# A two-layer decoder step on one core: side steps, weight splits and norms get other due times

## The chip, the cores and the metric

The kernel runs on one core of a Trainium2 chip. Its time is device time in microseconds (us) from launch to end; three runs of the kernel before took 2095.05, 2097.28 and 2099.48 us, median 2097.28. Engines: TensorE (PE, with its weight loads PEld), VectorE (DVE), ScalarE (ACT), GpSimd (POOL), and SyncE (SP), which here only issues DMAs.

## The reference, cut to what matters

One inference step of two layers for 1024 prompt positions and 8 single-position samples, together 1032 columns, all in float32 with a model width of 1024.

```python
def layer(x, ...):
    h = modulate(rmsnorm(x, g_mix), sh1, sc1)
    q, k, v, g, u, vv = split(h @ w_in)            # 4 heads x 128 each of q k v g, 4 groups x 128 each of u vv
    q, k = rope(q), rope(k) * 128 ** -0.5
    o, s_new = retention(q, k, v, s_ret)           # chunks of 128, decayed, state S carried on
    o_ret = silu(g) * group_norm(o) * gain
    o_gm = gelu(u) * (W_s @ layer_norm(gelu(vv)) + b_s)     # inside chunks of 128
    x = x + gt1 * (concat(o_ret, o_gm) @ w_out)
    h2 = modulate(rmsnorm(x, g_ffn), sh2, sc2)
    a = causal_dwconv3(h2 @ w_up)                  # 2 x 2048 columns
    x = x + gt2 * ((silu(a1) * a2) @ w_down)
# shifts, scales and gates (sh, sc, gt) are silu(c) @ w_ada + b_ada; two layers, then a last rmsnorm
```

## The kernel before, in words

Channels lie on partitions, the 1032 columns on the free axis in three chunks of 344. Every large product runs in three parts (`mm3`, L261): weights and activations are each split into a high part rounded for TensorE (`hi`, made on ScalarE, L212) and the rest (`lo`, made on VectorE, L221), and hi x hi, hi x lo and lo x hi are summed in PSUM. The three matmuls of one 128 x 128 weight tile are called a triple here.

A **unit** (L273) computes 128 output channels: three chunks of 8 triples, 24 in all. After each chunk VectorE evicts it from PSUM and multiplies by the norm's row factor R (L292); at the unit's end an eviction function `evac` works on the row. A layer has the value and key of head 0 in a **joint** (L296, two outputs at once, chunks in the order 2, 0, 1, evicted by ScalarE), then the query and gate of head 0, four units of head 1, two of group 0, two of group 1; an output product over three of the results (`partial`); heads 2 and 3, groups 2 and 3; another `partial`; and a `final_partial` (L511), which ends the residual chunk by chunk and sends each chunk's norm off while the next is computed. The feed-forward part is a joint and 30 units, in pairs, with partial products in between. That makes 52 units a layer.

**Side steps.** All smaller work is written as generators, `Task`s, which the planner `Side` (L55) lets go on between the triples. A unit calls `side.tick(KB)` after every third triple and at its end; that adds 1.31 to a clock that exists at build time only, and runs the next step of up to two tasks that are due, in the order of their priority and age. `yield y` makes a task's next step due y later; a task whose `after` is unfinished waits. In a joint a tick comes after each triple and counts as a third. So the planner sets only the order in which each engine's instructions stand; at run time an engine goes on as soon as its data are there. Instructions of one engine run in this order.

A head's tasks: `task_v` transposes v (L707, L630) and loads the old states; `task_k` rotates k (L675 to L677), transposes it (L630) into kt, scaled on ScalarE (L730), multiplies kt with v (L743) and sums the states S on VectorE; `task_q` rotates q, makes the masked scores `at` (L773) and the output o (L794, L796) and normalises it in `row_norm` (statistics L642, scale L645 to L654, normalise L657); `task_o` transposes o and os (L815, L630), multiplies by the gate and splits the result `mix`. Each of k, q and o comes after the ones before it. At the end of the key's and the query's units `rope_evac` puts three copies on ScalarE (L668 to L670). A group has `task_v` (transposes L850 and L630, the same row_norm, transpose of the last rows L858) and `task_s` (product with W_s, L873).

**Weights.** `Weights.ahead()` (L232) does what is next for the following unit: the low half of the piece whose high half is there, and the high half of the next. `high()` also issues the load of a piece two further on SyncE's queue. A unit calls it at triples 9, 15 and 21. Whatever is missing at the next unit's start is made then.

**Norms.** `norm` (L439) of a chunk: add the squares (VectorE, L378), sum over channels by matmul (`inv_rms`, L396, then a root on VectorE), write the factor to DRAM on GpSimd's queue, and read it back to all partitions on SyncE's. The three chunks' norms follow each other by `after`; the second has a wait of 8 at its head.

All these tiles share a pool of 23 buffers (`slot`), and all PSUM tiles eight banks. In layer 0 the conditioning weights (`ada`, product L590) pass through the same pool, at the lowest priority.

Of the kernel before, what the change touches and what calls it, by code (L numbers as in the profile page):

```python
# [41 lines left out]
ORDER = (2, 0, 1)  # L42
# [48 lines left out]
def tile_hybrid_decoder_step(  # L91
# [57 lines left out]
    for l in range(DEPTH):  # L149
# [15 lines left out]
        out, down = list(rows(w_out, OUT_GROUPS)), list(rows(w_down, DOWN_GROUPS))  # L165
# [107 lines left out]
    def unit(evac, R):  # L273

        u = W.get()
        a, b = None, small([128, 1], "wb", 4)
        for c in range(NC3):
            n, s = chunk(c, 2)
            ps = big()
            for k in range(KT):  # L280
                hi, lo = W.tile(u, k)
                mm3(ps[:, 0:n], hi, lo, Hh[:, k, s], Hl[:, k, s], k == 0, k == KT - 1)
                i = c * KT + k + 1
                if i in (9, 15, 21):
                    W.ahead()
                if i % 3 == 0 and i < NC3 * KT:
                    side.tick(KB)
            if c == 0:
                a = slot("row")
            if c == NC3 - 1:  # L290
                nc.scalar.activation(out=b, in_=ps[:, CW:CW + 1], func=ACTF.Copy)  # L291
            nc.vector.tensor_tensor(out=a[:, cols(c)], in0=ps[:, 0:CW], in1=R[:, cols(c)], op=ALU.mult)  # L292
        evac((a, b))
        side.tick(KB)
# [141 lines left out]
            late.append(lambda x=x, a=a, m=m: nc.vector.scalar_tensor_tensor(  # L436
                out=Hl[:, m, s], in0=x, scalar=a, in1=Hhf[:, m, s], op0=ALU.mult, op1=ALU.subtract))

    def norm(c, hold, R, A, B, gate=None, dma=True):  # L439

        n = CW if c < 2 else CW - NB
        if c == ORDER[1] and B is not mods[0][0]:
            yield 8
        rows = add_squares(c, hold, gate)
        yield 4
        w = inv_rms(rows)
        yield 4
        if dma:
            rd = to_dram(w)
        if c == 2 or not dma:  # L450
            r = spread(w, (3,) if dma else range(4))
        yield 1
        o = R[:, c * CW:c * CW + n]
        if dma:
            from_dram(o, rd)
        else:
            nc.scalar.activation(out=o, in_=r[:, 0:n], func=ACTF.Copy)
        if c == 2:
            q = small([128, KT, NB], "gs")
            ss = slice(SEQ, T)  # L460
            rb = r[:, CW - NB:CW].unsqueeze(1).to_broadcast([128, KT, NB])
            nc.vector.tensor_tensor(out=q, in0=XS, in1=rb, op=ALU.mult)
            nc.vector.tensor_tensor(out=q, in0=q, in1=A[:, :, 1:9], op=ALU.mult)
            nc.vector.tensor_tensor(out=q, in0=q, in1=B[:, :, 1:9], op=ALU.add)
            nc.scalar.activation(out=Hh[:, :, ss], in_=q, func=ACTF.Copy)
            nc.vector.tensor_tensor(out=Hl[:, :, ss], in0=q, in1=Hhf[:, :, ss], op=ALU.subtract)
# [44 lines left out]
    def final_partial(acts, gt, A, B=None, out=None):  # L511

        u = W.get(lazy=1)
        K = len(acts)
        norms = []
        R = None
        if out is None:
            R = rows_scale()
            columns(B)
        for o, c in enumerate(ORDER):  # L520
            n = CW if c < 2 else CW - NB
            s = slice(c * CW, (c + 1) * CW)
            hold, late = [], []
            for ms in GROUPS3:
                pss = {}
                mk = [(m, k) for m in ms for k in range(K)]
                if o == 0 and ms[0] == 0:
                    mk.sort(key=lambda q: q[1])
                for i, (m, k) in enumerate(mk):
                    hi, lo = W.tile(u, m * K + k)  # L530
                    if k == 0:
                        pss[m] = big()
                    ps = pss[m]
                    mm3(ps[:, 0:CW], hi, lo, acts[k][0][:, s], acts[k][1][:, s], k == 0, k == K - 1)
                    if k == K - 1:
                        xs = X[:, m, c * CW:c * CW + n]
                        nc.vector.scalar_tensor_tensor(  # L537
                            out=xs, in0=ps[:, 0:n], scalar=gt[:, m, 0:1], in1=xs, op0=ALU.mult, op1=ALU.add)
                        if c == 2:
                            nc.vector.tensor_tensor(out=ACS[:, m], in0=ps[:, n:CW], in1=ACS[:, m], op=ALU.add)  # L540
                    if i % K == K - 1 and i < len(mk) - 1:
                        side.tick(K * KB / 3)
                while late:
                    late.pop(0)()
                if out is None:
                    scaled(c, ms, A, late)
                squares(c, ms, hold, out is None or o < 2)
                if o == 0 and ms[0] == 0:
                    W[u[-1]]
                if o >= 1 and out is None:  # L550
                    W.ahead()
                side.tick(K * KB / 3)
            while late:
                late.pop(0)()
            gate = gt if c == 2 else None
            if out is not None:
                xg = v3(slot("xg"))
                for j, m in enumerate(GROUPS3[0]):
                    nc.scalar.activation(
                        out=xg[:, j, 0:n], in_=X[:, m, c * CW:c * CW + n], func=ACTF.Copy, scale=A[:, m:m + 1])  # L560
            norms.append(side.add(
                norm(c, hold, R, A, B, gate) if out is None else norm_out(c, hold, xg, A, out, gate),
                after=norms[-1:] if out is None else (), prio=0))
        return R, norms


# [52 lines left out]
    mods = [[mod[:, p if p < 5 else 5 + l] for p in range(6)] for l in range(DEPTH)]  # L619
# [40 lines left out]
    class Head:  # L660
# [61 lines left out]
        def task_k(self, sw):  # L722
            h = self.h
            yield 3
            self.rope(self.k, sw)
            kt = slot("kt")
            yield 4

            def ev(hf, ps):
                nc.scalar.activation(  # L730
                    out=kt[:, hf * 512:(hf + 1) * 512], in_=ps, func=ACTF.Identity, scale=dec[:, h:h + 1])
            halves(self.k, ev)
            yield 1.3
            vb = self.vb[:, 0:1024]
            vb8 = vb.rearrange("p (b e) -> p b e", b=8)
            nc.gpsimd.tensor_tensor(
                out=vb8, in0=vb8, in1=self.k[:, SEQ:T].unsqueeze(2).to_broadcast([128, 8, 128]), op=ALU.mult)
            self.S = slot("S")
            S = self.S[:, 0:1024].rearrange("p (c e) -> p c e", c=8)
            pss = [sps(), sps()]  # L740
            for q in range(8):
                t = slice(q * 128, (q + 1) * 128)
                nc.tensor.matmul(  # L743
                    pss[q // 4][:, q % 4 * 128:(q % 4 + 1) * 128], kt[:, t], self.vt[:, t], start=True, stop=True)
            for hf, ps in enumerate(pss):
                for q in range(4):
                    c = hf * 4 + q
                    kv = ps[:, q * 128:(q + 1) * 128]
                    if c == 0:
                        nc.vector.tensor_copy(S[:, 0], kv)  # L750
                    else:
                        nc.vector.scalar_tensor_tensor(
                            out=S[:, c], in0=S[:, c - 1], scalar=GAMMA[h] ** 128, in1=kv, op0=ALU.mult, op1=ALU.add)
            yield 3.5
            nc.gpsimd.dma_start(out=rp_o[self.l, h], in_=S[:, 7])
            s0 = self.S0[:, 0:1024]
            nc.vector.scalar_tensor_tensor(out=s0, in0=s0, scalar=GAMMA[h], in1=vb, op0=ALU.mult, op1=ALU.add)
            yield 2
            nc.gpsimd.dma_start(
                out=rs_o[self.l, h], in_=self.S0[:, 0:1024].rearrange("p (b e) -> p b e", b=8))  # L760

        def task_q(self, sw):
# [12 lines left out]
            for hf, ps in enumerate(pss):  # L775
                nc.vector.scalar_tensor_tensor(
                    out=at[:, hf * 512:(hf + 1) * 512].rearrange("p (c i) -> p c i", c=4),
# [7 lines left out]
                    start=(b % 2 == 0), stop=(b % 2 == 1), tile_position=(0, 32 * j))  # L785
            self.os = small([128, 128], "os")
            nc.scalar.activation(out=self.os, in_=ps[:, 0:128], func=ACTF.Copy)
            yield 2.5
            self.o = slot("o")
            pss = [sps(), sps()]  # L790
            for c in range(8):
                t = slice(c * 128, (c + 1) * 128)
                out = pss[c // 4][:, c % 4 * 128:(c % 4 + 1) * 128]
# [155 lines left out]
    with tc.manual_schedule():  # L949
# [16 lines left out]
        A, B = mods[0][1], mods[0][0]  # L966
# [10 lines left out]
        R = rows_scale()  # L977
# [33 lines left out]
        for l in range(DEPTH):  # L1011
# [26 lines left out]
            else:  # L1038
                joint(ev[:2], norms, ORDER, lambda c, i: side.drain(norms[0]), R)
            nc.gpsimd.affine_select(  # L1040
                out=wst, in_=wst, pattern=[[0, 4], [1, 128]], channel_multiplier=-1, base=0,
# [36 lines left out]
            R, norms = final_partial(a, gt1, mod[4], mod[3])  # L1078
# [17 lines left out]
            if l + 1 < DEPTH:  # L1096
                R, norms = final_partial(fs, gt2, mods[l + 1][1], mods[l + 1][0])
            else:
                _, norms = final_partial(fs, gt2, gf, out=yT)
# [94 lines left out]
```

## Time and profile before

| | |
|---|---|
| median of three runs | 2097.28 us |
| profiled execution | 2096.15 us |
| its span, first to last instruction | 2094.4 us |
| TensorE busy | 2032.0 us, 97% |
| VectorE busy | 1234.0 us, 59% |
| ScalarE busy | 669.3 us, 32% |
| GpSimd busy | 72.1 us, 3% |
| mean granted clock of TensorE | 0.990 |

How to read it: busy time of an engine is the time in which at least one of its instructions runs; matmuls overlap, so their starts are better to go by than their durations. A wait is idle time of an engine just ahead of an instruction, with the instruction that ended it behind the arrow. The granted clock is a share of full speed, 1.00 at 2.4 GHz and 0.50 at 1.2 GHz. Times of windows and timelines count from the span's start.

### The profile page before, as it was taken

The page shows a single profiled execution, that of the slowest core. Times are in us where ns is not written, and L with a number is a line of the kernel's source. Part 1 is how long each engine was busy: PE and PEld are TensorE (multiplying, and loading weights), DVE is VectorE, ACT ScalarE, POOL GpSimd, SP SyncE. Part 2 cuts the span into 40 slices and gives each one's busy share as a digit, 9 for nine tenths or more (in the row PEclk, how much of TensorE's full clock was granted, in tenths as well). Part 3 has the DMA queues.
Part 4 walks back from the last instruction along what each step waited for, and adds up shares of the span by engine and source line. Part 5 has one row for each costly group of instructions (what it writes and reads, how often), then busy time and mean ns, then how long its engine had stood idle before and what let it go on. Part 6 is the DMA issues. An engine that isn't in the chain of part 4 may idle for free.

```text
span 2094.4 us, 32628 instructions
## 1 busy us (share of the span) xinstructions
PE 2032.0 (97%) x13806; PEld 1976.5 (94%) x13806; DVE 1234.0 (59%) x2563; ACT 669.3 (32%) x927; POOL 72.1 (3%) x155
## 2 busy tenths in 40 slices
PE   7999999999999999999999999999999999999997
PEld 5988999999898999999999999999999999999997
DVE  5455635586555456555774564456857556646476
ACT  5332223234422322423343231233343322231432
POOL 0000000000000000000001000000100000000001
PEclk9999999999999999999999999999999999999998
DMA  9443111111554211110112210221111111111112
GB/s 371 165 147 126 56 67 51 46 65 32 211 192 170 91 51 41 41 59 33 64 58 76 72 41 31 72 72 41 52 48 61 41 51 45 47 41 51 41 34 82
DMA packets 51890, 164.33 MB, mean 78 GB/s; under 512 B 6864, under 2 KB 14384, under 8 KB 51744
## 3 DMA queue, kind: packets, MB, share of 16 engines
q1 hardware_dynamic: 47616, 151.22, 20.9%
q0 software_dynamic: 3728, 10.50, 1.4%
q8 instruction: 108, 1.77, 0.3%
q10 hardware_dynamic: 400, 0.53, 0.1%
q14 instruction: 38, 0.31, 0.1%
HBM read 152.88 MB, written 9.61 MB: 78 GB/s over the span
## 4 chain that ended last, share of the span: by engine, by line
PE 87%; DVE 7%; ACT 3%; DMA 1%; issue 1%; SPq 0%; DVEq 0%; ACTq 0%
PE big L262 27%; PE big L264 27%; PE big L263 26%; PE side L590 2%; PE side L630 1%; DVE X L537 1%; DVE Hl L436 1%; ACT Hh L435 1%; ACT sq L367 1%; PE side L743 1%; PE side L794 1%; PE side L873 1%; PE side L773 1%; DVE lo L221 1%; PE side L796 1%
## 5 line engine op out<-in xcount | busy, mean ns | idle before, releaser
L262 PE MATMUL big<-Hh,hi 128*128 128x344 f32 (+1 forms) x2688 | 877.4, 326 | 3.1 <-ACT Hh L435 2.0
L264 PE MATMUL big<-Hh,lo 128*128 128x344 f32 (+1 forms) x2688 | 867.7, 323 | 11.7 <-DVE lo L221 11.7
L263 PE MATMUL big<-Hl,hi 128*128 128x344 f32 (+1 forms) x2688 | 867.5, 323 | 1.0 <-DVE Hl L436 1.0
L262 PEld LDWEIGHTS big<-Hh,hi 128*128 128x128 f32 x2688 | 510.7, 190 | 20.7 <-issue 15.6
L264 PEld LDWEIGHTS big<-Hh,lo 128*128 128x128 f32 x2688 | 511.4, 190 | 12.8 <-DVE lo L221 12.8
L263 PEld LDWEIGHTS big<-Hl,hi 128*128 128x128 f32 x2688 | 511.1, 190 | 1.8 <-DVE Hl L436 1.7
L292 DVE TENSOR_TENSOR row<-big,R 128x344 f32<-128x344 f32 x312 | 160.2, 515 | 549.2 <-PE big L264 287.6
L336 DVE SCALAR_TENSOR_TENSOR X<-big,mod,X 128x344 f32<-128x344 f32 x384 | 211.7, 572 | 74.4 <-PE big L264 71.4
L262 PE MATMUL big<-ahi,hi 128*128 128x344 f32 x768 | 246.6, 321 | 0.0
L263 PE MATMUL big<-alo,hi 128*128 128x344 f32 x768 | 245.2, 319 | 0.0
L264 PE MATMUL big<-ahi,lo 128*128 128x344 f32 x768 | 245.2, 319 | 0.0
L291 ACT ACTIVATE wb<-big 128x1 f32<-128x1 f32 x104 | 17.5, 168 | 629.4 <-PE big L264 629.4
L221 DVE TENSOR_TENSOR lo<-raw,hi 128x1024 fp32r<-128x1024 f32 x160 | 195.0, 1219 | 15.5 <-ACT hi L212 14.3
L212 ACT ACTIVATE hi<-raw 128x1024 fp32r<-128x1024 f32 x160 | 166.0, 1048 | 6.6 <-PE big L263 4.4
L912 DVE SCALAR_TENSOR_TENSOR c<-row,pars,c 128x1032 f32<-128x1032 f32 x128 | 164.4, 1287 | 2.0 <-ACT acol L905 2.0
L262 PEld LDWEIGHTS big<-ahi,hi 128*128 128x128 f32 x768 | 144.3, 188 | 3.3 <-issue 1.6
L263 PEld LDWEIGHTS big<-alo,hi 128*128 128x128 f32 x768 | 144.4, 188 | 0.1
L264 PEld LDWEIGHTS big<-ahi,lo 128*128 128x128 f32 x768 | 144.3, 188 | 0.0
L262 PE MATMUL big<-hi,hi 128*128 128x344 f32 x384 | 123.7, 322 | 0.0
L264 PE MATMUL big<-hi,lo 128*128 128x344 f32 x384 | 122.7, 319 | 0.0
L263 PE MATMUL big<-lo,hi 128*128 128x344 f32 x384 | 122.6, 319 | 0.0
L938 ACT ACTIVATE ahi<-c 128x1032 fp32r<-128x1032 f32 x32 | 34.2, 1069 | 205.1 <-DVE c L936 183.4
(172 smaller groups left out, 1741.3 us busy)
## 6 DMA issues: line engine op xcount, KB each, us to landing
ada<-in_w_ada SPq DMA_DIRECT2D x96, 512.0 KB, 4.6
raw<-in_w_up SPq DMA_DIRECT2D x64, 512.0 KB, 3.5
raw<-in_w_in SPq DMA_DIRECT2D x48, 512.0 KB, 3.6
raw<-in_w_down SPq DMA_DIRECT2D x32, 512.0 KB, 3.5
raw<-in_w_out SPq DMA_DIRECT2D x16, 512.0 KB, 3.5
S<-in_s_ret POOLq DMA_DIRECT2D x8, 512.0 KB, 3.8
vb<-vd SPq DMA_DIRECT2D x8, 512.0 KB, 4.5
out_rs<-S POOLq DMA_DIRECT2D x8, 512.0 KB, 3.7
```

The costliest lines, as they stand in the source:

```text
L212: nc.scalar.activation(out=hi[:, 0:1024], in_=self.raw[i][:, 0:1024], func=ACTF.Copy)
L221: nc.vector.tensor_tensor(out=lo[:, 0:1024], in0=self.raw.pop(i)[:, 0:1024], in1=self.split[i][0].bitcast(F32)[:, 0:1024], op=ALU.subtract)
L262: nc.tensor.matmul(out, whi, rhi, start=start, stop=False)
L263: nc.tensor.matmul(out, whi, rlo, start=False, stop=False)
L264: nc.tensor.matmul(out, wlo, rhi, start=False, stop=stop)
L292: nc.vector.tensor_tensor(out=a[:, cols(c)], in0=ps[:, 0:CW], in1=R[:, cols(c)], op=ALU.mult)
L336: nc.vector.scalar_tensor_tensor(out=x, in0=ps[:, 0:CW], scalar=gt[:, m, 0:1], in1=x, op0=ALU.mult, op1=ALU.add)
L367: nc.scalar.activation(out=o, in_=x, func=ACTF.Square)
L435: nc.scalar.activation(out=Hh[:, m, s], in_=x, func=ACTF.Copy, scale=a)
L590: nc.tensor.matmul(ps[32 * j:32 * j + 32, 0:256], scond[:, k, :], w[:, j * 256:(j + 1) * 256], start=(k == 0), stop=(k == KT - 1), tile_po ...
L912: nc.vector.scalar_tensor_tensor(out=c[:, off:off + T], in0=a[:, 0:T], scalar=wt, in1=c[:, off:off + T], op0=ALU.mult, op1=ALU.add)
L938: nc.scalar.activation(out=hi[:, 0:T], in_=c2[:, 0:T], func=ACTF.Copy)
```

## The change

Four due times of a head's tasks grow; a unit calls `ahead` at triples 3, 8 and 21; the norms of the second and third chunk of a joint get waits of 9 and 5 at their head and 5 in place of 4 before the matmul, and the third chunk's norm no longer comes after the second's. No instruction is added or removed.

```diff
@@ unit
-                if i in (9, 15, 21):
+                if i in (3, 8, 21):
                     W.ahead()
@@ norm
-    def norm(c, hold, R, A, B, gate=None, dma=True):
+    def norm(c, hold, R, A, B, gate=None, dma=True, wait=0):
 
         n = CW if c < 2 else CW - NB
-        if c == ORDER[1] and B is not mods[0][0]:
-            yield 8
+        if wait:
+            yield wait
         rows = add_squares(c, hold, gate)
-        yield 4
+        yield 5 if wait else 4
         w = inv_rms(rows)
@@ final_partial
             norms.append(side.add(
-                norm(c, hold, R, A, B, gate) if out is None else norm_out(c, hold, xg, A, out, gate),
-                after=norms[-1:] if out is None else (), prio=0))
+                norm(c, hold, R, A, B, gate, wait=(0, 9, 5)[o]) if out is None else norm_out(c, hold, xg, A, out, gate),
+                after=norms[-1:] if out is None and o < 2 else (), prio=0))
@@ Head.task_k
             self.rope(self.k, sw)
             kt = slot("kt")
-            yield 4
+            yield 5
 ...
             halves(self.k, ev)
-            yield 1.3
+            yield 4
             vb = self.vb[:, 0:1024]
@@ Head.task_q
             nc.scalar.activation(out=self.os, in_=ps[:, 0:128], func=ACTF.Copy)
-            yield 2.5
+            yield 3.5
             self.o = slot("o")
```

## Rows read from the trace of the kernel before

**Rows 1.** The page: busy time of the engines; DMA issues, us to landing.
```profile
PE 2032.0 (97%) x13806; PEld 1976.5 (94%) x13806; DVE 1234.0 (59%) x2563; ACT 669.3 (32%) x927; POOL 72.1 (3%) x155
...
raw<-in_w_in SPq DMA_DIRECT2D x48, 512.0 KB, 3.6
```

**Rows 2.** Waits of PE: total us, times, longest us.
```profile
PE big L264 <- DVE lo L221: 11.7, 4, 3.3
PE side L743 <- ACT kt L730: 10.9, 6, 2.6
PE side L396 <- DVE sq L378: 9.5, 4, 3.0
PE side L590 <- DMA ada<-in_w_ada: 8.2, 7, 5.1
...
PE side L630 <- DVE row L677: 3.0, 2, 1.6
```

**Rows 3.** Windows: stretch, its us, busy per engine, granted clock, DMA share, GB/s.
```profile
404.60:411.30 6.70, 6.07 (x23) 6.01 (x24) 3.74 (x13) 1.16 (x1) 0.00 (x0) 0.50 0.00 0
503.60:506.90 3.30, 3.30 (x13) 3.30 (x12) 2.50 (x8) 0.00 (x0) 0.58 (x1) 0.50 0.00 0
...
194.30:204.30 10.00, 9.93 (x84) 8.61 (x84) 7.89 (x21) 3.18 (x3) 0.00 (x0) 1.00 0.74 260
```

**Rows 4.** Timeline of PE at 194 us: start, us, instruction, idle before it.
```profile
194.37 0.43 PE L264 MATMUL big<-Hh,lo 128*128 128x344 f32 x1 [2.02 <-DVE lo L221]
```

**Rows 5.** Timeline of PE at the joint of layer 0's feed-forward part.
```profile
498.60 0.32 PE L264 MATMUL big<-Hh,lo 128*128 128x346 f32 x1
498.76 0.32 PE L262 MATMUL big<-Hh,hi 128*128 128x346 f32 x1
...
502.32 0.65 PE L396 MATMUL side<-sq,ones_m 128*32 128x86 f32 x24 [2.93 <-DVE sq L378]
...
504.31 0.49 PE L262 MATMUL big<-Hh,hi 128*128 128x346 f32 x1
504.59 0.49 PE L263 MATMUL big<-Hl,hi 128*128 128x346 f32 x1
```

**Rows 6.** Timeline of ACT and PE behind head 2's query unit, layer 0.
```profile
298.95 1.06 ACT L670 ACTIVATE qs<-row 64x1032 f32<-64x1032 f32 x1
300.04 1.27 ACT L730 ACTIVATE kt<-side,dec 128x512 f32<-128x512 f32 x2
...
300.77 0.94 PE L743 MATMUL side<-vt,kt 128*128 128x128 f32 x6 [2.59 <-ACT kt L730]
```

**Rows 7.** Timeline of DVE in head 1's query unit, layer 0.
```profile
132.79 2.14 DVE L657 TENSOR_SCALAR o<-o,mv,fac 128x128 f32<-128x128 f32 x8
...
135.10 1.22 DVE L221 TENSOR_TENSOR lo<-raw,hi 128x1024 fp32r<-128x1024 f32 x1
...
138.64 1.23 DVE L677 TENSOR_TENSOR row<-row,ks 128x1032 f32<-128x1032 f32 x1
```

**Rows 8.** Timeline of DVE in group 2's u unit, layer 0.
```profile
394.15 0.52 DVE L292 TENSOR_TENSOR row<-big,R 128x344 f32<-128x344 f32 x1 [2.41 <-PE big L264]
...
399.17 2.12 DVE L657 TENSOR_SCALAR o<-o,mv,fac 128x128 f32<-128x128 f32 x8
...
401.46 0.70 DVE L645 BATCH_NORM_AGGREGATE mv<-st 128x2 f32<-128x6 f32 x9
...
403.95 1.22 DVE L221 TENSOR_TENSOR lo<-raw,hi 128x1024 fp32r<-128x1024 f32 x1
```

**Rows 9.** Timeline of ACT in one feed-forward unit of layer 1.
```profile
1713.41 1.04 ACT L212 ACTIVATE hi<-raw 128x1024 fp32r<-128x1024 f32 x1
1721.63 0.17 ACT L291 ACTIVATE wb<-big 128x1 f32<-128x1 f32 x1 [7.18 <-PE big L264]
```

**Rows 10.** Timeline of DVE at the joint of rows 5.
```profile
498.97 2.52 DVE L436 SCALAR_TENSOR_TENSOR Hl<-X,mod,Hh 128x344 fp32r<-128x344 f32 x5
501.40 0.87 DVE L378 TENSOR_TENSOR sq<-sq,sq 128x688 f32<-128x688 f32 x1
```

## The prediction

> **What bounds the kernel now.** First the page's busy line: TensorE is busy for 97% of the span, no other engine for over 59% (the first row of [rows 1]). So only TensorE's own idle time, and time in which it runs slowly, can be won. Next, TensorE's waits [rows 2]: four kinds of wait, which the change is aimed at, make up most of it. The next unit's low weight half came late 4 times (11.7 us), the copied key of a head 6 times (10.9 us), a norm's sum of squares at joints (9.5 us in 4, three of them at the joints), the rotated key 2 times (3.0 us). The wait for loads of the conditioning weights (8.2 us) lies almost wholly in the first 16 us, which the change doesn't touch. Third, the windows [rows 3]: behind the long stalls the granted clock is 0.50, the 1.2 GHz level, for a while (1.00 is 2.4 GHz). I count eight such stretches before the end, seven of at least 3.3 us and one of at least 6.7 us, 29.8 us together, each behind a stall of 2.6 us or more. Behind the stalls of 2.0 us and less the clock stayed at 1.00: the longest of them ended at 194.37 [rows 4], and the window from there on is the last of [rows 3]. Fourth, TensorE's timeline through one stall [rows 5]: matmuls start some 0.158 us apart before it (0.16 from 498.60 to 498.76) and 0.288 us apart in the half-clock stretch behind (0.28 from 504.31 to 504.59; both figures are means over some ten). So a stall costs itself and a slow tail.
>
> One triple (the three matmuls of one weight tile) takes 3 x 0.158 = 0.474 us, a unit's 24 triples 11.4 us. A side tick comes every 3 triples and counts as 1.31, so a step asked for after y comes at the first tick at which n x 1.31 reaches y.
>
> **The copied key (yield 1.3 to 4).** Before the change, the product with kt comes 1 tick behind the transposes, and its copy on ScalarE stands behind the three rotary copies of the query: the last of them starts at 298.95, the copy at 300.04, and TensorE stood 2.59 us until 300.77 [rows 6]. 4 asks for 4 ticks: 9 triples more, 4.3 us, against a longest wait of 2.6 us [rows 2]. All six go: -10.9 us. What is late next: the chain S, S0, query product, output, norm, mix of the same head all move by 9 triples, from the output on by 12 (2.5 to 3.5 is a step from 2 ticks to 3), in head 3 by 6 and 9, since there a budget clash falls away. GpSimd's product of k and v and its two stores of states move with them; nobody on TensorE waits for these. The mixes of heads 1 and 3 are still 30 and 81 triples ahead of the output products that read them.
>
> **The rotated key (yield 4 to 5).** This edit does nothing: 3 ticks are 3.93, 4 ticks 5.24, so both 4 and 5 mean 4 ticks. But its two stalls go by the others. VectorE began the rotation only after the previous head's normalise (132.79) and the low weight half (135.10), and ended it at 139.87 [rows 7]. The normalise now comes 12 triples later, behind the rotation, and the low half stands ahead of it. Of 12 triples (5.7 us) the rotation needs three operations, 3.6 us. -3.0 us.
>
> **Weights split at triples 3, 8, 21 instead of 9, 15, 21.** The four stalls are in the u unit of group 0 or 2: after the chunk's eviction at 394.15 VectorE has a head's scale, the group's statistics, the head's normalise (399.17) and the group's scale (401.46) before the low half (403.95), which ends 11.0 us after the eviction began; the two chunks left take TensorE 16 x 0.474 = 7.6 us [rows 8]. Now the low half stands ahead of that eviction, and the head's three steps come 9 to 12 triples later. All four go: -11.7 us. What is late next is the group's normalise at the unit's end with the head's normalise beside it: 2.3 + 2.3 us (399.17 to 401.46) and an eviction, some 6 us at most with what is left over; the first transpose that needs it comes 15 triples, 7.1 us, later. Covered by 1 us; I cost it at nothing, and up to 1 us four times if the cover is gone.
>
> What the edit costs elsewhere: the low half waits on VectorE for the high half on ScalarE, and the first chunk's eviction now waits behind it. In a feed-forward unit whose last chunk is done by 1721.63, and which so began about 1710.2, the high half ends at 1714.45, behind three eviction operations [rows 9]; then the low half, 1.2 us, to 1715.7, and only then the eviction of a chunk that was done 8 triples, 3.8 us, into the unit: some 2 us late, while the weights are needed at 1721.6. In a head's unit both key copies (1.3 us) and 0.7 us more of rotary copies come ahead: the low half is done about 8 us into 11.4. So 0; PSUM has eight banks, one per chunk of 3.8 us, and an eviction 2 to 4 us late blocks nobody. The high half's step also issues a weight load on SyncE's queue, now ahead of the broadcast load of v in the same tick; it is asked for two units, some 22 us, ahead and lands 3.6 us after issue (the second row of [rows 1]), so both have time.
>
> **Norms at the joint.** Norm of chunk 0: 8 becomes 9, so its sum of squares is issued at the joint's triple 3 rather than 1 (its wait begins with six ticks left before the joint, 7.86, and the joint's ticks are 0.437); 4 becomes 5, so its product comes 12 triples behind rather than 10: at triple 15, not 11. But the sum isn't waiting for its tick: VectorE is busy with the last low halves of the activations from 498.97 on and reaches it at 501.40 [rows 10]. It ends when it did, and TensorE arrives 4 triples, 1.90 us, later: the stall of 2.93 us [rows 5] shrinks to 1.03. Three joints: -5.7 us. The third chunk's norm no longer queues for the second: its sum is at triple 13, its product at 25, its row factor is asked for at 38, not 47. The row scale behind the joint may start earlier; TensorE wasn't waiting for it, so 0.
>
> **The slow clock.** With every stall in question at 1.1 us or less, all eight half-clock stretches should go: 29.8 x (1 - 0.158/0.288) = 13.4 us. The Trainium skill, page "TensorE: Matmul & The Clock Gate" (Terms), prices throttled time at one minus the clock's share, here half: 14.9 us; the rows' spacing gives less and I keep the rows. The same page (What's actually happening) says that the count of slow matmuls differs between runs of one kernel; by that the joints' short stalls might still drop the clock, which no row here shows for so short a stall.
>
> **Slots.** 23 buffers of one tag serve weights, heads and, in layer 0, the conditioning weights. Heads 0 and 1 hold six or seven of them for 4 to 6 us longer, so a load may get its buffer later. Bounds: 0 (before the change, no such wait after the start, [rows 2]), and 8 us, four late steps of 2 us; nothing below 0, since nothing is freed earlier that TensorE waits for. I take 1.
>
> **Sum.** 10.9 + 3.0 + 11.7 + 5.7 = 31.3 us of idle, 13.4 us of clock, less 1: 43.7. The profiled execution took 2096.15 (span 2094.4), so 2052.5; the median of the runs, 2097.28, lies 1.1 above it: 2053.5. The end and the first 50 us stay as they are.
>
> **Rivals.**
> A. Half the gain: the stalls shift. VectorE's clump moves from the group's unit to the one behind, or the key's copy is late at the later place too (head 2's mix now falls between head 3's rotation and that copy). For: four stalls came from just such a clump [rows 8]. Against: VectorE is idle for 41% of the span. With the four waits on the low half coming back at other places, 2.9 us each, and a slow tail of 1.5 us on average (13.3 us of half clock x 0.451 over four): 4 x 4.4 = 17.6, so 2071.
> B. The clock falls at the joints for all that: 3 x 3.3 x 0.451 = 4.5 us, 2058. For: the stalls there are shortened, not gone. Against: stalls up to 2.02 us were without it.
> C. The buffers: layer 0's loads and the head's tiles wait, 8 us and with slow tails up to twice that, 2061 to 2068.
> D. Slower. The low half stands at the head of VectorE's queue, with eviction behind it, in all 104 units. Chain per unit: eviction, ScalarE's three operations, high half, low half, the rest of VectorE's work. In [rows 9] the high half ends 4.3 us into the unit; behind it come the low half, two convolution taps and three evictions, 5.3 us of the 7.1 left. In the other unit of a pair a product and an activation's low half come on top, 2.4 us at the low half's 1.2: 0.6 us too many. If the loop is over 11.4 us in most units, it accumulates until the low half is what TensorE waits for: from 0.42 us per unit on (43.7 over 104) the gain is gone; at 0.6 us, 2053.5 + 62 = 2116. Against: the first unit of each pair has 1.8 us to spare and gives the lateness back.
>
> **How the numbers follow.** Chances: forecast 0.62 (its own range 2047 to 2058), A 0.14, B 0.09, C 0.07, D 0.05, and 0.03 that the steps move and the time does not. 0.2% (4 us) is about what a measurement can tell from no change. Faster: forecast, A, B, C, 0.92; same 0.03; slower 0.05. Range 2045 to 2073: below, the joints' remains (3.1 us) and the allowance also go, with the runs' scatter; above, A.
>
> **What would show it.** TensorE's waits without the rows for kt, the rotated key and the low weight half; the wait on L378 at 3 to 4 us in place of 9; granted clock 1.00 in every window from 100 to 2000 us; the page's TensorE busy time down by some 14 us and its idle by 31. Wrong would be: a new row on L264, L743 or L858, waits on loads in layer 0, or a clock of 0.5 behind a stall of 1 us.

## The result, and the profile after

The changed kernel takes 2058.48 us, the median of 4 runs (2057.46 to 2059.40), against 2096.16 for 4 runs of the kernel before beside them: a ratio of 0.9823 [0.9800, 0.9845], so 37.7 us or 1.8% less. The forecast was 2053.5, its own range 2047 to 2058, the whole range 2045 to 2073. The time lies 0.5 us above the forecast's own range and inside the whole one. The direction and the bulk of the gain hold; 5 us are missing, and the experiments below show where they are.

First the busy line of the page after (busy us, share of the span, instructions), against the first row of [rows 1]. The profiled execution took 2059.40 us with a span of 2057.7; before, it was 2096.15 with 2094.4.

```profile
PE 2020.6 (98%) x13806; PEld 1967.9 (96%) x13806; DVE 1231.1 (60%) x2563; ACT 668.1 (32%) x927; POOL 70.1 (3%) x155
```

The same 13806 matmuls were busy for 11.4 us less. Most of that is time at the low clock: six of eight slow stretches are gone (below), which is some 10.3 us (the 13.4 of the forecast less 3.1 for the two that are left). For the other 1.1 us no cause is shown. What is left of the span is TensorE's idle time: 2094.4 - 2032.0 = 62.4 us before, 2057.7 - 2020.6 = 37.1 after, 25.3 less. The forecast had 13.4 and 31.3.

Then TensorE's waits after (total us, times, longest us), against [rows 2].

```profile
PE side L590 <- DMA ada<-in_w_ada: 9.2, 8, 5.2
PE side L743 <- ACT kt L730: 4.7, 2, 2.3
PE side L409 <- DVE rw L361: 4.1, 2, 3.9
PE side L396 <- DVE sq L378: 3.1, 3, 1.1
PE big L263 <- DVE alo L940: 2.4, 1, 2.4
```

The reader should look for the rows that are missing, for those that shrank, and for those that are new. The low weight half on L264 (11.7 us) and the rotated key on L630 (3.0) are gone. The joints' norm on L396 fell from 9.5 to 3.1. The copied key on L743 fell only from 10.9 to 4.7. A row is new: the first partial product of the feed-forward part, L263, waits 2.4 us for alo, the low half of the activations, made on L940. The loads on L590 cost 1.0 more, one new wait that ends at 157.08; the allowance for buffers had this size, but that a buffer came free late is not shown.

Third, the windows after (stretch, its us, then PE, PEld, DVE, ACT, POOL busy, granted clock, DMA share, GB/s). The first two lie behind the stalls of layer 1 at the copied key and at alo, the third behind the key's stall of layer 0, the fourth behind a joint's.

```profile
1362.00:1365.30 3.30, 3.30 (x15) 3.30 (x15) 2.99 (x7) 0.07 (x1) 0.00 (x0) 0.50 0.26 71
1560.00:1563.30 3.30, 3.30 (x12) 3.30 (x13) 1.60 (x4) 2.57 (x4) 0.00 (x0) 0.50 0.43 154
356.00:366.00 10.00, 9.93 (x67) 9.93 (x68) 5.94 (x13) 3.09 (x6) 1.13 (x2) 1.00 0.32 113
488.00:498.00 10.00, 9.95 (x102) 9.48 (x103) 5.17 (x19) 1.20 (x4) 1.29 (x4) 1.00 0.23 72
```

Of the eight stretches at 0.50 (1.2 GHz) before the end, [rows 3], two are left, both new in place. They follow the two long stalls of layer 1; the equal stall of layer 0 at 356 did not lower the clock. At the joint, whose stall ended at 488.05, it stays at 1.00.

Fourth, TensorE's timeline at one of the two key stalls and at the new one (start, us, instruction, idle before it and what ended it).

```profile
356.07 0.60 PE L743 MATMUL side<-vt,kt 128*128 128x128 f32 x3 [2.32 <-ACT kt L730]
...
1559.94 0.66 PE L263 MATMUL big<-alo,hi 128*128 128x344 f32 x1 [2.38 <-DVE alo L940]
```

Now the cause of the first, on VectorE in the query unit of head 3, layer 0, in which the key is rotated (same columns).

```profile
341.69 1.23 DVE L221 TENSOR_TENSOR lo<-raw,hi 128x1024 fp32r<-128x1024 f32 x1 [4.54 <-ACT hi L212]
...
343.26 1.22 DVE L675 TENSOR_TENSOR row<-row,cos 128x1032 f32<-128x1032 f32 x1
...
346.81 1.40 DVE L812 SCALAR_TENSOR_TENSOR mix<-side,pars,row 128x512 f32<-128x512 f32 x2
...
349.86 1.24 DVE L189 TENSOR_TENSOR lo<-mix,hi 128x1032 fp32r<-128x1032 f32 x1 [1.13 <-ACT hi L188]
351.01 0.93 DVE L292 TENSOR_TENSOR row<-big,R 128x344 f32<-128x344 f32 x2
```

And ScalarE behind it, same head.

```profile
351.98 1.16 ACT L668 ACTIVATE row<-row,wb 128x1032 f32<-128x1032 f32 x1 [2.09 <-DVE row L292]
...
355.33 1.27 ACT L730 ACTIVATE kt<-side,dec 128x512 f32<-128x512 f32 x2
```

VectorE stood 4.54 us at the low half, which waited for ScalarE's high half. The key's rotation came behind it (343.26), then head 2's mix and its low half (346.81 to 351.1). Only then came the query's last two evictions (351.01). ScalarE waited 2.09 us for these, scaled the query row at 351.98, made the query's copies after it, and reached the copy of the key at 355.33. TensorE had been ready since 353.75, 2.32 us before its product started.

The new wait on alo, on VectorE in layer 1, has the same shape.

```profile
1551.98 1.22 DVE L221 TENSOR_TENSOR lo<-raw,hi 128x1024 fp32r<-128x1024 f32 x1 [3.42 <-ACT hi L212]
...
1554.75 1.23 DVE L936 TENSOR_TENSOR c<-c,c 128x1032 f32<-128x1032 f32 x1
...
1557.52 1.22 DVE L221 TENSOR_TENSOR lo<-raw,hi 128x1024 fp32r<-128x1024 f32 x1
1558.65 1.23 DVE L940 TENSOR_TENSOR alo<-c,ahi 128x1032 fp32r<-128x1032 f32 x1
```

Last, the row of VectorE's own waits that ties the two together (total us, times, longest): before,

```profile
DVE lo L221 <- ACT hi L212: 14.3, 6, 4.1
```

and after.

```profile
DVE lo L221 <- ACT hi L212: 300.1, 88, 5.8
```

The early low half makes VectorE stand for ScalarE in 88 of its 160 executions, 300 us in all. VectorE is busy for only 60% of the span, so nearly all of it is free; by the two timelines it costs where something that TensorE needs soon stands behind. That this is the cause, and not only beside it, is for the experiments.

### The profile page after: what moved, and what is told of

Read it like the earlier page. It is cut to its first block, busy times and chain, and to the rows that moved or that the text cites. A ratio compares the mean times of both kernels' runs of the same rounds, so it can differ in the third digit from the quotient of the medians.

```text
span 2057.7 us, 32589 instructions
## 1 busy us (share of the span) xinstructions
PE 2020.6 (98%) x13806; PEld 1967.9 (96%) x13806; DVE 1231.1 (60%) x2563; ACT 668.1 (32%) x927; POOL 70.1 (3%) x155
## 4 chain that ended last, share of the span: by engine, by line
PE 89%; DVE 6%; ACT 3%; DMA 1%; issue 0%; SPq 0%; DVEq 0%; ACTq 0%
PE big L262 27%; PE big L263 27%; PE big L264 27%; PE side L590 2%; PE side L630 1%; DVE X L537 1%; DVE Hl L436 1%; ACT Hh L435 1%; ACT sq L367 1%; DMA ada<-in_w_ada 1%; PE side L743 1%; PE side L873 1%; PE side L794 1%; PE side L773 1%; PE side L796 1%; DVE sq L371 1%
## 5 line engine op out<-in xcount | busy, mean ns | idle before, releaser
L263 PE MATMUL big<-Hl,hi 128*128 128x344 f32 (+1 forms) x2688 | 863.8, 321 | 1.0 <-DVE Hl L436 1.0
L264 PE MATMUL big<-Hh,lo 128*128 128x344 f32 (+1 forms) x2688 | 863.5, 321 | 0.0
L263 PEld LDWEIGHTS big<-Hl,hi 128*128 128x128 f32 x2688 | 508.2, 189 | 1.8 <-DVE Hl L436 1.7
L264 PEld LDWEIGHTS big<-Hh,lo 128*128 128x128 f32 x2688 | 508.4, 189 | 0.0
L221 DVE TENSOR_TENSOR lo<-raw,hi 128x1024 fp32r<-128x1024 f32 x160 | 195.6, 1222 | 300.1 <-ACT hi L212 300.1
L263 PE MATMUL big<-alo,hi 128*128 128x344 f32 x768 | 246.3, 321 | 2.4 <-DVE alo L940 2.4
L264 PE MATMUL big<-ahi,lo 128*128 128x344 f32 x768 | 246.1, 320 | 0.0
L291 ACT ACTIVATE wb<-big 128x1 f32<-128x1 f32 x104 | 17.4, 168 | 587.3 <-PE big L264 587.3
L263 PEld LDWEIGHTS big<-alo,hi 128*128 128x128 f32 x768 | 144.9, 189 | 2.6 <-DVE alo L940 2.6
L264 PEld LDWEIGHTS big<-ahi,lo 128*128 128x128 f32 x768 | 144.8, 189 | 0.0
L264 PE MATMUL big<-hi,lo 128*128 128x344 f32 x384 | 122.8, 320 | 0.0
L263 PE MATMUL big<-lo,hi 128*128 128x344 f32 x384 | 122.7, 320 | 0.0
```

The source lines that it names most:

```text
L221: nc.vector.tensor_tensor(out=lo[:, 0:1024], in0=self.raw.pop(i)[:, 0:1024], in1=self.split[i][0].bitcast(F32)[:, 0:1024], op=ALU.subtract)
L263: nc.tensor.matmul(out, whi, rlo, start=False, stop=False)
L264: nc.tensor.matmul(out, wlo, rhi, start=False, stop=stop)
```

## The experiments

The theory: the due times and the norms bring the whole gain; the early low half loses some 5 us of it, by standing at the head of VectorE's queue. The rival: the split is needed for the low half's 11.7 us, as the prediction had it, and the kernel would lose them without it. The change was first taken apart into three, each alone on the kernel before.

**The split alone (x_ahead).**

```
-                if i in (9, 15, 21):
+                if i in (3, 8, 21):
```

> The kernel before with the weight split alone moved to triples 3, 8, 21. Theory (in the changed kernel the early low half does two things: it takes the four waits on the low weight half away, and it makes VectorE stand idle for ScalarE's high half with work queued behind it, which is where the new wait on an activation's low half in layer 1 comes from): the row L264 <- lo L221 goes (11.7 us, and 6.0 us of its slow tails), L630 <- L677 falls from 3.0 to under 0.5 us since the low half no longer stands ahead of the rotation, a wait on alo L940 of about 2.4 us appears, VectorE's idle time ahead of L221 rises from 15 us to 250 us or more; kt's 10.9 us and the joints' 9.5 us stay. Together some 2096 - 17 = 2079 us, ratio 0.992. Rival (the alo wait comes from the joint's norms or the heads' due times): no row on alo, 2075 us.

Measured: 2094.61 (2092.39 to 2097.36), ratio 1.0001 [0.9992, 1.0011]. The expected 2079 is missed: no gain where 17 us were expected. TensorE's waits in it:

```profile
PE side L743 <- ACT kt L730: 12.1, 6, 2.6
...
PE side L396 <- DVE sq L378: 9.0, 3, 3.0
PE side L630 <- DVE row L677: 5.8, 2, 3.0
...
PE big L263 <- DVE alo L940: 2.2, 1, 2.2
PE big L262 <- ACT ahi L938: 2.1, 1, 2.1
```

The row on L264 is gone, so the split does remove the 11.7 us, even alone. It gives most of them back: the rotated key takes 5.8 in place of 3.0, the copied key 12.1 in place of 10.9, and both halves of the activations are late, 4.3 us together, in the first partial product of the feed-forward part. The expectation had the rotated key under 0.5, with the low half out of the rotation's way. But in head 1's query unit the low half waits 2.79 us for ScalarE (until 130.74) with head 0's scale and normalise queued behind it, and the rotation comes only at 137.60. That leaves 11.7 - 2.8 - 1.2 - 4.3 = 3.4 us of idle won in this execution, of which the median shows nothing. VectorE's idle time ahead of L221 is 227.4 us (expected: 250 or more). The low clock stays as it was: eight stretches at 0.50, seven of 3.4 us and one of 6.8.

**The due times alone (x_due).**

```
-            yield 4
+            yield 5
...
-            yield 1.3
+            yield 4
...
-            yield 2.5
+            yield 3.5
```

> The kernel before with the heads' due times alone (yields 5, 4 and 3.5). Theory (the later head steps take away the waits on kt, on the rotated key and, since a head's scale and normalise leave the group's unit, most of those on the low weight half; the low half at triple 15 has 5.8 us of VectorE work ahead of it where 7.6 us are left, in head 3's case 7.6): kt 10.9 to 0 us, rotated key 3.0 to 0, low half 11.7 to under 1, joints' 9.5 as before; with the tails of 9 us some 2096 - 34 = 2062 us, ratio 0.984. No wait on kt in head 3, since VectorE doesn't idle ahead of the rotation there. Rival 1 (the split's place is needed for the low half): L264 <- L221 stays at 8 us or more, 2074 us. Rival 2 (head 2's mix alone makes head 3's key late): L743 <- kt 4 to 5 us in 2, 2068 us.

Measured: 2064.42 (2062.28 to 2066.80), ratio 0.9853 [0.9837, 0.9868]. TensorE's waits:

```profile
PE side L590 <- DMA ada<-in_w_ada: 10.5, 9, 5.3
PE side L396 <- DVE sq L378: 9.3, 4, 3.0
...
PE side L743 <- ACT kt L730: 1.7, 2, 0.9
```

Neither L264 nor L630 is in the list. So the low half's stalls go without the split. VectorE's timeline in the unit of [rows 8] shows how (start, us, instruction):

```profile
393.40 1.22 DVE L221 TENSOR_TENSOR lo<-raw,hi 128x1024 fp32r<-128x1024 f32 x1
...
397.94 2.14 DVE L657 TENSOR_SCALAR o<-o,mv,fac 128x128 f32<-128x128 f32 x8
```

The head's normalise now comes behind the low half, not ahead of it. The copied key falls to 1.7 us, less than the 4.7 that the whole change leaves, but not to the 0 that was expected: head 3 keeps 0.84 and 0.85 us, one stall in each layer, without any early low half. These three edits bring 30 of the 38 us. The first of them (4 to 5) has no part in that: with it put back, the changed kernel builds to the same program, so every engine has the same instructions in the same order.

**The norms alone (x_norm).**

```
-        if c == ORDER[1] and B is not mods[0][0]:
-            yield 8
+        if wait:
+            yield wait
...
-        yield 4
+        yield 5 if wait else 4
...
-                norm(c, hold, R, A, B, gate) if out is None else norm_out(c, hold, xg, A, out, gate),
-                after=norms[-1:] if out is None else (), prio=0))
+                norm(c, hold, R, A, B, gate, wait=(0, 9, 5)[o]) if out is None else norm_out(c, hold, xg, A, out, gate),
+                after=norms[-1:] if out is None and o < 2 else (), prio=0))
```

> The kernel before with the joints' norms alone. Theory: only L396 <- L378 falls, from 9.5 to 3.1 us in 3, with three slow stretches of 3.4 us (4.6 us of time) gone: 2096 - 11 = 2085 us, ratio 0.995. Rival (the later product also shifts the chunks behind it into another wait): L396 falls but a wait on rw, R or alo of 2 us or more appears, 2088 us or more.

Measured: 2082.76 (2079.17 to 2085.31), ratio 0.9941 [0.9927, 0.9956]. TensorE's waits:

```profile
PE big L264 <- DVE lo L221: 11.6, 4, 3.2
PE side L743 <- ACT kt L730: 10.9, 6, 2.6
...
PE side L396 <- DVE sq L378: 4.1, 4, 1.1
```

The wait on L396, 9.5 us, becomes 4.1, of which 1.0 is the start's; the other rows that the change is aimed at stay. The norms are worth about twice these 5.4 us. This execution had three half-clock stretches in place of eight behind the first 50 us: the three at the joints are gone, and two fewer stand behind stalls that the norms have nothing to do with (see the last section). Inside the first 50 us it had one of some 10 us, from 17.6 on, which the kernel before had not.

**The whole change without the split (y_noahead).**

```
-                if i in (3, 8, 21):
+                if i in (9, 15, 21):
```

> The changed kernel with the weight split back at triples 9, 15, 21 (due times and norms as changed). Theory (the early low half causes both new waits): kt's 4.7 us in head 3 and alo's 2.4 us go with their two slow stretches, the waits on the low weight half come back by under 1 us in two places; 2058.5 - 9 = 2049 us, faster than the changed kernel, 0.977 of the one before. Rival 1 (head 2's mix causes head 3's late key, the norms the alo): both stay, 2058 us. Rival 2 (the split's place is what removed the waits on the low half): L264 <- L221 at 8 us or more, 2066 us or more.

Measured: 2053.58 (2053.13 to 2053.94), ratio 0.9803 [0.9788, 0.9818]: faster than the change by about 5 us, not slower, though not the 2049 expected: the theory had the copied key go wholly, and 1.7 us of it stay, as in x_due. Its waits on the copied key and the joints:

```profile
PE side L396 <- DVE sq L378: 3.4, 4, 1.1
...
PE side L743 <- ACT kt L730: 1.7, 2, 0.8
```

No row for L264 and none for alo. VectorE in the same head, with the low half behind the rotation now:

```profile
339.68 1.23 DVE L675 TENSOR_TENSOR row<-row,cos 128x1032 f32<-128x1032 f32 x1 [1.50 <-ACT ks L670]
...
343.24 1.22 DVE L221 TENSOR_TENSOR lo<-raw,hi 128x1024 fp32r<-128x1024 f32 x1
344.38 1.40 DVE L812 SCALAR_TENSOR_TENSOR mix<-side,pars,row 128x512 f32<-128x512 f32 x2
```

The rotation starts at 339.68, not 343.26, and all behind it is 2.4 us earlier (the mix at 344.38, not 346.81). In this trace the whole unit is 0.9 us earlier: ScalarE's small copy at the end of the key's unit (L291) starts at 333.86, in the changed kernel at 334.76. The 1.5 us that remain are what the stall on the copied key loses, 2.3 to 0.8 us. The parts add up: the due times alone save 30.0 us (2094.37 - 2064.42), the norms 11.6, together 41.6, and the two in one kernel 40.8. The split then costs 4 to 5 us: 2058.48 - 2053.58 = 4.9, and the ranges of the two kernels' runs lie apart.

**The change again, beside the kernels that follow (after_again).** No edit.

> The changed kernel once more, beside the next three on one chip. Both theories: 2058.5 us, the same waits (kt 4.7, alo 2.4, joints 3.1 us). What may differ is the clock behind the stalls: before this, stalls of 2.3 to 3.2 us were followed by a half-clock stretch in some executions and not in others, so between none and three stretches of 3.4 us.

Measured: 2057.88 (2056.06 to 2059.43), ratio 0.9828 [0.9814, 0.9842]: the first result again, with the same waits and two half-clock stretches behind the stalls, not all in the same places (last section).

**The high half early, the low half late (z_lowlate).** This parts the two halves of the split: ScalarE's step stays at triple 3, VectorE's goes back to 15.

```
-                if i in (3, 8, 21):
+                if i in (3, 15, 21):
```

> The changed kernel with the high half early and the low half late: triples 3, 15, 21. Theory (the place of the low half in VectorE's queue is what hurts, since VectorE runs its queue in order and idles there for ScalarE's high half): like the kernel with 9, 15, 21, 2053.6 us; no wait on alo, kt at 1.7 us, VectorE's idle time ahead of L221 back from 300 us to under 40. Rival (the early high half hurts, through ScalarE's order or the buffers it holds): kt 4.7 and alo 2.4 us stay, 2058.5 us.

Measured: 2053.35 (2053.21 to 2054.80), ratio 0.9809 [0.9795, 0.9822], as without the split. TensorE's waits, then VectorE's:

```profile
PE side L743 <- ACT kt L730: 1.6, 2, 0.8
```

```profile
DVE lo L221 <- ACT hi L212: 19.0, 11, 3.1
```

The 300.1 us of VectorE are 19.0 again, the row for alo is gone, the copied key is at 1.6. The kernel is 4.5 us faster than the changed one measured beside it (2057.88). So it is the low half's place in VectorE's queue that costs the 5 us; the early high half on ScalarE alone costs nothing that shows.

**The output's due time back (z_os25).** On the changed kernel without the split, the step 2.5 to 3.5 is undone.

```
-            yield 3.5
+            yield 2.5
```

> The kernel with 9, 15, 21 and all other changes, but the output product's yield back from 3.5 to 2.5. Theory (that edit only moves the head's last steps by 3 triples, and the wait on kt's copy is what was won): kt as without it, the low half's row at most 0.4 us in two places (its VectorE queue then holds 7.6 us where 7.6 us are left), 2054 us, the same within 0.1%. Rival (those 3 triples are what freed the group's unit): L264 <- L221 at 3 us or more, 2058 us or more.

Measured: 2064.49 (2062.67 to 2065.61), ratio 0.9859 [0.9845, 0.9873]: 11 us slower than with 3.5, where no difference was expected. The rival, a wait on L264, does not come either. TensorE's waits:

```profile
PE side L743 <- ACT kt L730: 6.0, 2, 3.5
...
PE side L630 <- DVE row L677: 3.6, 2, 1.8
```

The 6.0 us on the copied key are in head 1, at 147.23 and 1166.10. VectorE at the end of its query unit, layer 0:

```profile
139.87 2.15 DVE L657 TENSOR_SCALAR o<-o,mv,fac 128x128 f32<-128x128 f32 x8
...
142.59 0.93 DVE L292 TENSOR_TENSOR row<-big,R 128x344 f32<-128x344 f32 x2
```

Head 0's normalise stands ahead of the query's last eviction (the first of the two at 142.59); ScalarE's row scale waits for it until 143.13, and the copy of the key comes at 146.49. With 3.5 (y_noahead) the last eviction starts at 136.76, ahead of the normalise at 137.19, and the copy at 140.67, in a unit whose end (ScalarE's L291) is 0.5 us earlier.

The 3.6 us on the rotated key are in head 3, at 352.29 and 1364.17. VectorE in its query unit, layer 0:

```profile
344.40 1.41 DVE L812 SCALAR_TENSOR_TENSOR mix<-side,pars,row 128x512 f32<-128x512 f32 x2 [1.92 <-PE side L630]
...
347.45 1.23 DVE L189 TENSOR_TENSOR lo<-mix,hi 128x1032 fp32r<-128x1032 f32 x1 [1.13 <-ACT hi L188]
348.60 1.23 DVE L675 TENSOR_TENSOR row<-row,cos 128x1032 f32<-128x1032 f32 x1
```

Three triples, 1.4 us, decide which of two steps that fall due close together is issued first: the previous head's mix, with 1.13 us of waiting for ScalarE ahead of its low half, or the rotation that TensorE needs next. With 2.5 the mix stands first, and the rotation starts at 348.60, 10.5 us behind ScalarE's copy at the end of the key's unit (L291, 338.15); with 3.5 (y_noahead) it starts 5.8 us behind it (339.68 and 333.86).

**A better one (z_best).** Without the split, and the two waits that are left asked for one unit's tick (1.31) later.

```
-                if i in (3, 8, 21):
+                if i in (9, 15, 21):
...
-        yield 5 if wait else 4
+        yield (4, 5, 6.5)[(wait > 0) + (wait == 9)]
...
-            yield 4
+            yield 5.3
```

> The kernel with 9, 15, 21 and the changed due times and norms, and two more delays: 5.3 in place of 4 ahead of the product with kt (5 ticks) and 6.5 in place of 5 ahead of the joint's first late norm product (15 triples, so it stands at triple 18 in place of 15). Theory (each wait is as long as its step stands too early): the joints' 3.1 us go to 0 (1.1 us wanted, 1.4 given), kt's 1.7 us to 0 (0.85 wanted, 1.4 given), the group's L858 0.8 us too: 2053.6 - 5 = 2049 us. Rival (another wait takes their place, as the head's last steps now fall on the group's normalise): joints to 0, but L858, L850 or L264 at 1.5 us or more, 2051 to 2056 us.

Measured: 2047.96 (2047.80 to 2048.16), ratio 0.9781 [0.9768, 0.9795]: 10 us faster than the change, and the fastest of all. Its waits:

```profile
PE side L850 <- ACT row L831: 2.5, 3, 0.9
...
PE side L396 <- DVE sq L378: 0.9, 1, 0.9
```

The copied key is gone, and of the joints' norm only the start's stall is left. The time lies 1 us under the 2049 expected. The rival's new wait came too, smaller than its price: the group's row on L850, 2.5 us in three, 0.8 to 0.9 us at a time.

## Why the prediction was right, and where it was not

*The low half on L264*: 11.7 predicted, 11.7 measured. But the prediction gave it all to the split. The due times alone remove it, and so does the split alone; the prediction named both causes (the low half ahead of the eviction, the head's three steps later) and did not ask whether one was enough. That is why it took the split to be worth 11.7 us, when without it the kernel is faster.

*The copied key*: 10.9 predicted, 6.2 measured. *The step that failed is "What the edit costs elsewhere ... So 0"*: "an eviction 2 to 4 us late blocks nobody". It followed the early low half into a feed-forward unit and a head's unit by the weights' due time and by PSUM's banks, where no wait shows indeed, and never asked what else TensorE needs from the instructions queued behind it on VectorE. Its figure for the low half itself was right: done about 8 us into a head's unit, measured 342.92, 8.2 us behind the copy at 334.76. But in the query units of head 3 that lateness passes through the rotation, the mix, the query's evictions and ScalarE's row scale to the copy. It makes some 1.5 of the 2.3 us that are left of the stall in each layer, 3.0 of the 4.7. The other 1.7 us stay without the split too (x_due, y_noahead): there "All six go" failed by itself. It set 4.3 us more against the longest wait and took the copy to come when it did; in head 3 the previous head's mix and its low half stand ahead of the query's last evictions, and the copy is 0.85 us late at the later place. The prediction had seen that head 2's mix falls there, and used it only for rival A.

*A new wait on alo*: 0 predicted, 2.4 measured, from the same step. Rival D named the mechanism (the low half at the head of VectorE's queue, eviction behind it) but let it decide in all 104 units by accumulation. It shows in three places, the key stall of each layer and this one, and no wait on the low half came back anywhere.

*The rotated key*: 3.0 and 3.0, by the other edits, as said; the edit of 4 to 5 does nothing. The step from 2.5 to 3.5, which has no price of its own in the prediction, is worth 11 us beside the other edits (z_os25). *The joints*: 1.03 us each predicted, 1.03 to 1.05 measured. The sum of squares ended when it did, and TensorE came 4 triples later; 5.7 us predicted, 5.8 measured (3.1 left of 8.9); the start's norm gave 0.6 more, for which the prediction had no term. *Buffers*: an allowance of 1, measured 1.0 on L590 in layer 0, its cause not shown.

*The clock*: 13.4 predicted, from 29.8 us of low clock to none before the end; measured, two stretches were left and TensorE's busy time fell by 11.4. At the rows' spacing the two, of 3.4 us each, cost 2 x 3.4 x 0.451 = 3.1 us. So the 7.0 us by which the profiled execution misses the predicted saving (43.7 less 36.75) are 4.7 of the copied key, 2.4 of alo and 2.0 of TensorE's busy time (13.4 less 11.4), less 0.7 that the norms brought more and some 1.4 of small gaps. That no slow stretch would be left rested on a limit read from one execution, stalls of 2.0 us and less without one; the last section shows that this limit does not hold. The two stretches that stayed stand behind stalls that the prediction did not have.

Of the rivals, B did not come: no clock of 0.50 at a joint. That its 2058 is the measured time is chance. C did not come either, beyond the allowance. Of A's two places one was right, the key's copy late at the later place too; the waits on the low half, which made its price of 17.6 us, did not come back.

## What to carry to other kernels

An instruction that is moved earlier in the queue of an engine that runs it in order brings its wait along, even where the engine has time to spare: before giving it a cost of nothing, list what stands behind it in that queue in each kind of unit, and which engine waits for that. Split a producer from its follow-up on another engine and move only the one that doesn't wait (here the high half may go early, the low half not). When two edits would each remove the same stall, price each of them alone before the sum.

## What the runs showed of the hardware

Whether a stall is followed by a stretch at 1.2 GHz is not set by its length in these runs. With the norms alone (x_norm), the clock stayed up behind the longest stall of the four on the low half and fell behind a shorter one on the copied key. TensorE's timeline of that kernel:

```profile
146.34 0.49 PE L743 MATMUL side<-vt,kt 128*128 128x128 f32 x2 [1.94 <-ACT kt L730]
...
405.01 0.43 PE L264 MATMUL big<-Hh,lo 128*128 128x344 f32 x1 [3.23 <-DVE lo L221]
```

and the windows behind them:

```profile
147.40:150.70 3.30, 3.30 (x15) 3.30 (x15) 2.61 (x7) 1.36 (x2) 0.00 (x0) 0.50 0.15 26
...
405.00:415.00 10.00, 9.99 (x66) 9.95 (x67) 8.55 (x23) 3.18 (x3) 0.00 (x0) 1.00 0.00 0
```

After 1.94 us it is 0.50, after 3.23 us 1.00. In the kernel before, the same two stalls went the other way round: 1.92 us, ending at 146.62, was followed by 1.00, and 3.23 us, ending at 405.23, by 0.50 [rows 3]. In x_due a stretch at 0.50 even stands behind a stall of 1.05 us, which ended at 50.69. The prediction had read from one execution that the clock falls behind 2.6 us or more and holds behind 2.0 or less; these refute it. Two executions of the same changed kernel differ as well: in the first the stalls at 1361 and 1560 were followed by 0.50 and the one at 356 was not; in the second (after_again), those at 355 and 1362 were, and that before 1561, 2.38 us long, was not:

```profile
355.40:358.70 3.30, 3.17 (x15) 3.17 (x16) 1.67 (x3) 1.60 (x3) 0.00 (x0) 0.50 0.02 5
...
1561.40:1564.70 3.30, 3.30 (x23) 3.30 (x22) 2.27 (x6) 2.68 (x4) 0.00 (x0) 1.00 0.35 139
```

The Trainium skill, page "TensorE: Matmul & The Clock Gate" (What's actually happening), says that the count of slow matmuls at a kernel's start changes between runs of one kernel. Here the same shows behind stalls in the middle, of which that passage does not speak.

So a stall costs itself and, now and then, a tail of some 3.4 x 0.451 = 1.5 us. The scatter of the times fits this. All kernels have one stall of 3.9 us some 10 us before the end. Those whose other stalls behind the start are about 1.1 us or less lie, in four runs each, within 0.4 us (2047.80 to 2048.16, z_best), 0.8 us (2053.13 to 2053.94, y_noahead) and 1.6 us (2053.21 to 2054.80, z_lowlate). The kernel before spreads over 9 us in four runs (2090.51 to 2099.48) and 12 in 17 (2089.49 to 2101.92), the changed one over 3.4 in five (2056.06 to 2059.43). A single profile of a kernel with many such stalls gives its clock's part only to a few us, and taking out stalls went with a steadier kernel as well as a faster one, as far as so few runs tell. What sets whether a given stall lowers the clock stays open.
